# Scattering the experts' results: one copy and plain float32 products in place of two rounded halves

## The chip, the cores and the metric

The kernel runs on one core of one Trainium2 chip. The metric is the time of one execution on the device, in microseconds (us). Before the change it is 1255.69 us, the median of three runs (1255.01 to 1255.78).

## What is computed

Two layers of a decoder trunk on 256 tokens of width 1024. The change touches the second layer's experts: eight SwiGLU networks, of which each token uses two.

```python
logits = (xt @ w_router).astype(jnp.float32)
top_v, top_i = lax.top_k(logits, TOP_K)
gates = jax.nn.softmax(top_v, axis=-1)
gate = jnp.sum(jax.nn.one_hot(top_i, N_EXPERTS, dtype=jnp.float32) * gates[..., None], axis=1)
y = jnp.zeros_like(xt)
for e in range(N_EXPERTS):
    y = y + gate[:, e:e + 1].astype(xt.dtype) * swiglu(xt, wg[e], wu[e], wd[e])
```

with `swiglu(h) = (silu(h @ wg) * (h @ wu)) @ wd`, 1024 to 3584 to 1024. A residual add and a final RMSNorm follow.

## The kernel before, in words

All float32 precision on TensorE comes from halves. A value is split into `hi`, its copy rounded to the type float32r (ScalarE, L145 and L177), and `lo`, the rest (VectorE, L146 and L182). A product of two split operands is three matmuls (`mm3`, L154 to L158). Other products are plain float32 matmuls, without halves.

The experts (`moe`) run on gathered tokens. For each expert a one-hot matrix `pm` (tokens by slots) is built, the tokens are gathered by matmuls with it (`Group.gather`, L625), and the expert's result is scattered back to the tokens by matmuls with its transpose `pT` (`Job.turn_mask`, `evac_mask`). There are two kinds of job, ordered by the number of tokens that fell to an expert:

- **Wide** (5 jobs): up to 128 tokens; its products are split (L158, tile 128*128, three matmuls of 512 columns each). Its result `y` stands in two banks `psS`, one for each half `nb` of the 1024 columns.
- **Narrow** (3 jobs): up to 64 tokens; its products are plain float32 with 64 output columns on the array (L756 up, L772 down, tile 128*64), so that two run side by side. Its result stands in one bank `psA`: rows 0 to 63 hold the first 512 columns, rows 64 to 127 the second.

Each job has seven chunks (512 hidden channels each). `run` lays the chunks of wide and narrow jobs into one list of steps, in the order that a table fixes in the code: a step is one half of a weight piece (1 MB, loaded by SyncE into a ring of 12 buffers). The order is written out by hand on PE, VectorE and ScalarE; each engine takes its instructions strictly as they stand.

After the last chunk of a job the result leaves PSUM and is scattered. `evac_y` (L659) splits it into `yh` (ScalarE) and `yl` (VectorE). `scatter` takes a bank and multiplies both halves by `pT`, adding up in PSUM: for a wide job at L685 with the full array, for a narrow job at L714 with 64 rows, so that the scatters of the two `nb` run side by side. `add` (L667, VectorE) multiplies by the gate and adds to the tokens `xs`. In `run` (L826 to L838) these are placed at the steps after the job's end, `e0`: `evac` of half `nb` at `e0` and `e0+2`, the scatters one step apart (narrow jobs: two in a step), the adds behind them. So the scatters of a job lie between the matmuls of whatever chunk comes next, wide or narrow. There are two `psS` banks: the first two scatters take over those of `y`, the third takes the one that the first `add` gives back, and so on.

The very last job is narrow, with nothing to hide behind. It uses `evac_plain` (L701): one copy of the result, half of it by ScalarE, half by VectorE, and one plain float32 matmul for each scatter (L710).

A part of the program behind a branch (L1035) serves experts with more tokens than their room; it is not entered in these runs.

Of the kernel before, what the change touches and what calls it, by code (L numbers as in the profile page):

```python
# [10 lines left out]
F32 = mybir.dt.float32  # L11
F32R = mybir.dt.float32r
BF16 = mybir.dt.bfloat16
I32 = mybir.dt.int32
AF = mybir.ActivationFunctionType
# [4 lines left out]
P = 128  # L20
# [57 lines left out]
def hybrid_kernel(ctx: ExitStack, tc: tile.TileContext, x_d, xT_d, cst_d, fin_d, router_d,  # L78
                  wpool_d, win_d, wout_d, ffn_d, moe_d, out_d):
    nc = tc.nc  # L80
# [22 lines left out]
    def nm(s):  # L103
        uid[0] += 1
        return f"{s}_{uid[0]}"
# [4 lines left out]
    def bank_a():  # L110
        return bank("A", 4)

    def bank_s():
        return bank("S", 2)
# [59 lines left out]
    def split_evac(*parts):  # L174
        for hi, lo, src, g in parts:
            if g is None:
                nc.scalar.activation(hi, src, AF.Copy)  # L177
            else:
                nc.scalar.activation(hi, src, AF.Copy, scale=g)
        for hi, lo, src, g in parts:  # L180
            if g is None:
                nc.vector.tensor_tensor(lo, src, hi.bitcast(F32), op=ALU.subtract)  # L182
            else:
                nc.vector.scalar_tensor_tensor(lo, src, g, hi.bitcast(F32), op0=ALU.mult, op1=ALU.subtract)  # L184
# [287 lines left out]
    def moe(l, pool, acc, close):  # L472
# [22 lines left out]
        def add(t, nb):  # L495
            v = xs[:, t, nb * 512:(nb + 1) * 512]
            nc.vector.tensor_tensor(v, v, acc[nb, t], op=ALU.add)
# [143 lines left out]
        class Job:  # L641
# [14 lines left out]
                self.pT = pool.tile([P, NT * P], F32R, tag=self.kind + "pT", name=nm("pT"), bufs=1)  # L656
                nc.scalar.activation(self.pT, self.tb[:, 0:NT * P], AF.Copy)

            def evac_y(self, nb):  # L659
                yh = pool.tile([P, 512], F32R, tag="ah", name=nm("yh"), bufs=2)  # L660
                yl = pool.tile([P, 512], F32R, tag="al", name=nm("yl"), bufs=2)
                split_evac((yh, yl, self.y[nb], None))
                self.yp[nb] = yh, yl

            def add(self, nb, t):
                xv = xs[:, t, nb * 512:(nb + 1) * 512]
                nc.vector.scalar_tensor_tensor(xv, self.banks.pop((nb, t)), self.gate_col(t), xv, op0=ALU.mult, op1=ALU.add)  # L667
# [1 line left out]
        class Wide(Job):  # L669
# [4 lines left out]

            def start(self):
                self.y = [bank_s() for nb in range(2)]
                self.yp = {}

            def evac(self, nb):
                self.evac_y(nb)  # L680

            def scatter(self, nb, t):
                b = self.banks[nb, t] = bank_s()
                for i in range(2):
                    nc.tensor.matmul(b, self.pT[:, t * P:(t + 1) * P], self.yp[nb][i], start=i == 0, stop=i == 1)  # L685

        class Narrow(Job):

# [3 lines left out]

            def start(self):
                self.y = [bank_a()]
                self.yp = {}

            def evac(self, nb):
                if nb == 0:
                    self.evac_y(0)

            def evac_plain(self):  # L701
                self.yf = pool.tile([P, 512], F32R, tag="ah", name=nm("yf"), bufs=2).bitcast(F32)
                nc.scalar.activation(self.yf[:, 0:256], self.y[0][:, 0:256], AF.Copy)
                nc.vector.tensor_copy(self.yf[:, 256:512], self.y[0][:, 256:512])

            def scatter(self, nb, t, plain=False):
                b = self.banks[nb, t] = bank_a()
                rows = slice(nb * HP, (nb + 1) * HP)
                if plain:
                    nc.tensor.matmul(b, self.pT[rows, t * P:(t + 1) * P].bitcast(F32), self.yf[rows, :], start=True,  # L710
                                     stop=True)
                    return
                for i in range(2):
                    nc.tensor.matmul(b, self.pT[rows, t * P:(t + 1) * P], self.yp[0][i][rows, :], start=i == 0, stop=i == 1)  # L714

        class Chunk:

# [57 lines left out]
        def run(items, gathers, pieces=(), extra=(), small_ops=iter(())):  # L775


            chunks = [Chunk(job, c) for job, c in items]
# [18 lines left out]
            end = len(steps)  # L797
            before, after = {}, {}
# [7 lines left out]
            for n, ch in enumerate(chunks):  # L806
                b, job = pos["g", n, 0], ch.job
# [18 lines left out]
                if ch.c == NC_E - 1 and not final:  # L826
                    e0 = pos["d", n, 3] + 1
                    for i in range(4):
                        if job.splits:
                            nb, t = divmod(i, 2)  # L830
                            s = e0 + 1 + i
                        else:
                            t, nb = divmod(i, 2)
# [11 lines left out]
                        then(b + 7 + j, lambda j=j, made=made: made[0].gather(j))  # L845
                        at(b + 8 + j, lambda j=j, made=made: made[0].evac(j))

            last = chunks[-1].job
            plain = () if last.splits else (True,)
            for i, f in enumerate([(last.evac, (nb,)) for nb in range(2)] if last.splits else [(last.evac_plain, ())]):  # L850
                before.setdefault(end, []).insert(i, f)
            for when, s, f in extra:
                when = {"at": at, "then": then}[when]
                when(s, f)
# [37 lines left out]
            job = chunks[-1].job  # L892
            for t in range(NT):
                for nb in range(2):
                    job.scatter(nb, t, *plain)
                    job.add(nb, t)


# [136 lines left out]
        with tc.If(n_most > 0):  # L1035
            nc.vector.tensor_scalar(slot[:, :, 0], slot[:, :, 0], float(P), None, op0=ALU.subtract)
            with tc.For_i(0, NE) as e:
# [4 lines left out]
                with tc.If(n_e > 0):  # L1042
                    sg_ = small.tile([P, 2, NT], F32, tag="slot_gate", name="slot_gate")
                    for t in range(NT):
                        nc.vector.tensor_copy(sg_[:, 0, t:t + 1], slot[:, t, ds(e, 1)])
                        nc.vector.tensor_copy(sg_[:, 1, t:t + 1], gate[:, t, ds(e, 1)])
                    job = Wide(lambda c, i: moe_d[ds(e, 1), c, i].rearrange("a p d -> p (a d)"),
                               lambda t: sg_[:, 0, t:t + 1], lambda t: sg_[:, 1, t:t + 1])
# [70 lines left out]
    with tc.tile_pool(name="moe", bufs=2, reuse_waits="tile") as pool, \  # L1119
            tc.tile_pool(name="more", bufs=MORE_BUFS, reuse_waits="tile") as extra:  # L1120
        more.append(extra)
        moe_pool.append(pool)
        moe(1, pool, acc, close)
# [89 lines left out]
```

## Time and profile before

| | |
|---|---|
| median of three runs | 1255.69 us |
| the profiled execution | 1256.09 us |
| its span in the trace | 1254.3 us |
| PE (matmul) busy | 1238.4 us, 99% |
| PE weight loads busy | 971.9 us, 77% |
| VectorE (DVE) busy | 845.5 us, 67% |
| ScalarE (ACT) busy | 704.2 us, 56% |
| DMA, mean over the span | 334 GB/s |

The span is what the profiler saw of the execution, from its first to its last instruction; the execution's own time holds 1.8 us more around it. Matmuls are pipelined, so the time of one record is longer than the distance to the next: what a matmul costs is read from the distance of starts or ends. A float32 matmul of the program stands in the trace as two records, a matmul on rounded halves as one.

### The profile page before, as it was taken

Reading aid. Unit: us, or ns where it says so; the run is one execution under the profiler, and the core shown is the slowest. Engines: PE = TensorE matmul, PEld = TensorE weight load, DVE = VectorE, ACT = ScalarE, POOL = GpSimd, SP = SyncE. Lnnn points to the kernel's source line nnn. Section 1 sums busy time; section 2 is a strip of 40 time slices with the busy share of each in tenths; the row PEclk is TensorE's granted clock in tenths of the full one; section 3 lists DMA queues with packets and bytes.
Section 4 is the critical chain, followed back from the end, with each engine's and each line's share of the span. In section 5 each row is a group of like instructions: output and inputs, shape, how many; then the busy total and the mean of one; then the engine's idle time right before and its main releaser. Section 6 shows DMA issues by size and latency. Waiting matters only on the chain.

```text
span 1254.3 us, 19056 instructions
## 1 busy us (share of the span) xinstructions
PE 1238.4 (99%) x7217; PEld 971.9 (77%) x7217; DVE 845.5 (67%) x1152; ACT 704.2 (56%) x917; POOL 18.1 (1%) x34
## 2 busy tenths in 40 slices
PE   9999999999999999999999999999999999999996
PEld 7989999989987777777777677777777677777772
DVE  5786555556869768676766677765865687567663
ACT  6466444456458756555666556655664565556541
POOL 1010000000000000000000000000000000000000
PEclk9999999999999999999999999999999999999998
DMA  9745555545254999999999999999999999999980
GB/s 367 302 143 197 177 198 188 183 167 202 101 201 159 421 421 421 420 421 421 421 399 421 419 410 406 375 421 421 415 408 421 390 416 420 397 420 421 421 368 36
DMA packets 59428, 418.32 MB, mean 334 GB/s; under 512 B 6848, under 2 KB 6976, under 8 KB 9280
## 3 DMA queue, kind: packets, MB, share of 16 engines
q1 hardware_dynamic: 58464, 415.43, 82.2%
q8 instruction: 58, 0.95, 0.3%
q10 hardware_dynamic: 720, 1.07, 0.2%
q0 software_dynamic: 144, 0.52, 0.1%
q14 instruction: 42, 0.34, 0.1%
HBM read 415.95 MB, written 1.05 MB: 332 GB/s over the span
## 4 chain that ended last, share of the span: by engine, by line
PE 96%; ACT 1%; DVE 1%; issue 0%; DMA 0%; POOL 0%; SPq 0%; ACTq 0%; POOLq 0%
PE psA L158 45%; PE psS L158 25%; PE psA L756 12%; PE psA L772 6%; PE psT L733 2%; PE psT L625 1%; PE psS L685 1%; PE psS L270 1%; ACT hi L145 1%; PE psT L193 0%; DMA raw<-in_win 0%; DVE lo L146 0%; PE psT L318 0%; ACT junk L161 0%; PE psT L380 0%
## 5 line engine op out<-in xcount | busy, mean ns | idle before, releaser
L146 DVE TENSOR_TENSOR lo<-raw,hi 128x1024 fp32r<-128x1024 f32 x534 | 639.8, 1222 | 272.9 <-ACT hi L145 259.9
L145 ACT ACTIVATE hi<-raw 128x1024 fp32r<-128x1024 f32 x534 | 553.2, 1058 | 222.6 <-PE psA L158 123.2
L158 PE MATMUL psA<-hi,xh 128*128 128x512 f32 x560 | 223.6, 399 | 0.1
L158 PE MATMUL psA<-lo,xh 128*128 128x512 f32 x560 | 218.9, 391 | 0.5 <-DVE lo L146 0.5
L158 PE MATMUL psA<-hi,xl 128*128 128x512 f32 x560 | 218.5, 390 | 0.0
L756 PE MATMUL psA<-raw,xn 128*64 128x256 f32 x1344 | 152.0, 381 | 0.0
L756 PEld LDWEIGHTS psA<-raw,xn 128*64 128x64 f32 x1344 | 94.2, 137 | 55.9 <-issue 9.9
L158 PEld LDWEIGHTS psA<-hi,xh 128*128 128x128 f32 x560 | 105.2, 188 | 31.9 <-issue 10.9
L158 PEld LDWEIGHTS psA<-lo,xh 128*128 128x128 f32 x560 | 105.1, 188 | 23.7 <-DVE lo L146 1.2
L158 PEld LDWEIGHTS psA<-hi,xl 128*128 128x128 f32 x560 | 105.3, 188 | 20.5 <-DVE xl L184 0.2
L725 ACT ACTIVATE a<-psA 128x512 f32<-128x512 f32 (+1 forms) x56 | 29.0, 518 | 163.6 <-PE psA L756 146.6
L158 PE MATMUL psS<-hi,ah 128*128 128x512 f32 x280 | 112.2, 401 | 0.0
L158 PE MATMUL psS<-lo,ah 128*128 128x512 f32 x280 | 109.6, 391 | 0.0
L158 PE MATMUL psS<-hi,al 128*128 128x512 f32 x280 | 109.5, 391 | 0.0
L158 PE MATMUL psS<-hh,hi 128*128 128x256 f32 x320 | 89.9, 281 | 0.0
L158 PE MATMUL psS<-hh,lo 128*128 128x256 f32 x320 | 89.9, 281 | 0.0
L158 PE MATMUL psS<-hl,hi 128*128 128x256 f32 x320 | 89.8, 281 | 0.0
L772 PE MATMUL psA<-raw,aT 128*64 128x512 f32 x336 | 76.7, 598 | 0.0
L158 PEld LDWEIGHTS psS<-lo,ah 128*128 128x128 f32 x280 | 52.6, 188 | 12.2
L158 PEld LDWEIGHTS psS<-hh,lo 128*128 128x128 f32 x320 | 61.3, 192 | 0.0
L158 PEld LDWEIGHTS psS<-hi,ah 128*128 128x128 f32 x280 | 52.7, 188 | 10.5 <-issue 0.4
L158 PEld LDWEIGHTS psS<-hi,al 128*128 128x128 f32 x280 | 52.7, 188 | 10.0
(213 smaller groups left out, 1460.8 us busy)
## 6 DMA issues: line engine op xcount, KB each, us to landing
raw<-in_moe SPq DMA_DIRECT2D x336, 1024.0 KB, 10.4
raw<-in_ffn SPq DMA_DIRECT2D x33, 1024.0 KB, 4.9
raw<-in_win SPq DMA_DIRECT2D x14, 1024.0 KB, 4.9
raw<-in_wout SPq DMA_DIRECT2D x8, 1024.0 KB, 10.0
raw<-in_win SPq DMA_DIRECT2D x4, 512.0 KB, 6.9
raw<-in_xT SPq DMA_DIRECT2D x4, 256.0 KB, 6.1
xs<-in_x SPq DMA_DIRECT2D x2, 512.0 KB, 12.0
out<-o ACTq DMA_DIRECT2D x4, 256.0 KB, 2.7
```

What stands on the lines that cost most here:

```text
L145: nc.scalar.activation(hi, v, AF.Copy)
L146: nc.vector.tensor_tensor(lo, v, hi.bitcast(F32), op=ALU.subtract)
L158: nc.tensor.matmul(out, lhs, rhs, start=first and i == 0, stop=last and i == 2)
L270: nc.tensor.matmul(banks[i][:, c0:c0 + k1], q[:, q0:q0 + P], k[:, 0:k1], start=True, stop=True)
L625: nc.tensor.matmul(bank[:, i * 256:i * 256 + self.n], part[:, t, k * P:(k + 1) * P], self.pm[:, t, 0:self.n], start=n == 0, stop=n == 3)
L685: nc.tensor.matmul(b, self.pT[:, t * P:(t + 1) * P], self.yp[nb][i], start=i == 0, stop=i == 1)
L725: nc.scalar.activation(self.a, self.g[:, 0:self.n], AF.Silu)
L733: nc.tensor.transpose(self.tb[:, j * P:(j + 1) * P], self.a[:, j * P:(j + 1) * P], ident)
L756: nc.tensor.matmul(bank[half * HP:(half + 1) * HP, 0:256], self.job.xg[:, k, :], w[:, c:c + 256], start=k == 0, stop=k == NK - 1)
L772: nc.tensor.matmul(y[0][nb * HP:(nb + 1) * HP, :], self.aT[:, c:c + HP], w[:, nb * 512:(nb + 1) * 512], start=first, stop=last)
```

## The change

`evac_y` goes. A wide job's result is copied once: the first 512 columns by ScalarE, the second by VectorE, each into one float32 tile (`yf`). A narrow job's is copied as `evac_plain` did it. Every scatter is one plain float32 matmul of `pT` with `yf`. The last job's special case is no longer special. The matrices are the same: `pT` still has the type float32r and is read as float32.

```diff
--- before.py
+++ after.py
@@ -656,12 +656,6 @@
                 self.pT = pool.tile([P, NT * P], F32R, tag=self.kind + "pT", name=nm("pT"), bufs=1)
                 nc.scalar.activation(self.pT, self.tb[:, 0:NT * P], AF.Copy)
 
-            def evac_y(self, nb):
-                yh = pool.tile([P, 512], F32R, tag="ah", name=nm("yh"), bufs=2)
-                yl = pool.tile([P, 512], F32R, tag="al", name=nm("yl"), bufs=2)
-                split_evac((yh, yl, self.y[nb], None))
-                self.yp[nb] = yh, yl
-
             def add(self, nb, t):
                 xv = xs[:, t, nb * 512:(nb + 1) * 512]
                 nc.vector.scalar_tensor_tensor(xv, self.banks.pop((nb, t)), self.gate_col(t), xv, op0=ALU.mult, op1=ALU.add)
@@ -674,15 +668,18 @@
 
             def start(self):
                 self.y = [bank_s() for nb in range(2)]
-                self.yp = {}
+                self.yf = [None, None]
 
             def evac(self, nb):
-                self.evac_y(nb)
+                self.yf[nb] = pool.tile([P, 512], F32R, tag=("ah", "al")[nb], name=nm("yf"), bufs=2).bitcast(F32)
+                if nb == 0:
+                    nc.scalar.activation(self.yf[nb], self.y[nb], AF.Copy)
+                else:
+                    nc.vector.tensor_copy(self.yf[nb], self.y[nb])
 
             def scatter(self, nb, t):
                 b = self.banks[nb, t] = bank_s()
-                for i in range(2):
-                    nc.tensor.matmul(b, self.pT[:, t * P:(t + 1) * P], self.yp[nb][i], start=i == 0, stop=i == 1)
+                nc.tensor.matmul(b, self.pT[:, t * P:(t + 1) * P].bitcast(F32), self.yf[nb], start=True, stop=True)
 
         class Narrow(Job):
 
@@ -692,26 +689,17 @@
 
             def start(self):
                 self.y = [bank_a()]
-                self.yp = {}
 
             def evac(self, nb):
                 if nb == 0:
-                    self.evac_y(0)
-
-            def evac_plain(self):
-                self.yf = pool.tile([P, 512], F32R, tag="ah", name=nm("yf"), bufs=2).bitcast(F32)
-                nc.scalar.activation(self.yf[:, 0:256], self.y[0][:, 0:256], AF.Copy)
-                nc.vector.tensor_copy(self.yf[:, 256:512], self.y[0][:, 256:512])
-
-            def scatter(self, nb, t, plain=False):
+                    self.yf = pool.tile([P, 512], F32R, tag="ah", name=nm("yf"), bufs=2).bitcast(F32)
+                    nc.scalar.activation(self.yf[:, 0:256], self.y[0][:, 0:256], AF.Copy)
+                    nc.vector.tensor_copy(self.yf[:, 256:512], self.y[0][:, 256:512])
+
+            def scatter(self, nb, t):
                 b = self.banks[nb, t] = bank_a()
                 rows = slice(nb * HP, (nb + 1) * HP)
-                if plain:
-                    nc.tensor.matmul(b, self.pT[rows, t * P:(t + 1) * P].bitcast(F32), self.yf[rows, :], start=True,
-                                     stop=True)
-                    return
-                for i in range(2):
-                    nc.tensor.matmul(b, self.pT[rows, t * P:(t + 1) * P], self.yp[0][i][rows, :], start=i == 0, stop=i == 1)
+                nc.tensor.matmul(b, self.pT[rows, t * P:(t + 1) * P].bitcast(F32), self.yf[rows, :], start=True, stop=True)
 
         class Chunk:
 
@@ -845,10 +833,8 @@
                         then(b + 7 + j, lambda j=j, made=made: made[0].gather(j))
                         at(b + 8 + j, lambda j=j, made=made: made[0].evac(j))
 
-            last = chunks[-1].job
-            plain = () if last.splits else (True,)
-            for i, f in enumerate([(last.evac, (nb,)) for nb in range(2)] if last.splits else [(last.evac_plain, ())]):
-                before.setdefault(end, []).insert(i, f)
+            for nb in range(2):
+                before.setdefault(end, []).insert(nb, (chunks[-1].job.evac, (nb,)))
             for when, s, f in extra:
                 when = {"at": at, "then": then}[when]
                 when(s, f)
@@ -892,7 +878,7 @@
             job = chunks[-1].job
             for t in range(NT):
                 for nb in range(2):
-                    job.scatter(nb, t, *plain)
+                    job.scatter(nb, t)
                     job.add(nb, t)
```

On PE, at the end of the second wide job, the first of its four scatters among the next wide job's up projection; before the change (`psA` is the gate or up bank of the next chunk, `hi`/`lo` the weights, `xh`/`xl` its tokens, `psS` the scatter's bank):

```order
L158 MATMUL psA_6886<-lo_6941,xh_6026 128x512
L685 MATMUL psS_6976<-yh_6956,pT_6062 128x512
L685 MATMUL psS_6976<-yl_6957,pT_6062 128x512
L158 MATMUL psA_6991<-hi_6952,xh_6026 128x512
L158 MATMUL psA_6991<-hi_6952,xl_6027 128x512
L158 MATMUL psA_6991<-lo_6953,xh_6026 128x512
```

Here two rows multiply `pT` by the two halves; three more matmuls on `psA` follow before the next such pair. On PE at the same place with the change:

```order
L158 MATMUL psA_6873<-lo_6928,xh_6018 128x512
L682 MATMUL psS_6961<-yf_6943,pT_6054 128x512
L158 MATMUL psA_6973<-hi_6939,xh_6018 128x512
L158 MATMUL psA_6973<-hi_6939,xl_6019 128x512
L158 MATMUL psA_6973<-lo_6940,xh_6018 128x512
```

The pair with `yh` and `yl` has become one row with `yf`; the matmuls around it, and their number between two scatters, stay.

On VectorE at the same place, from the evacuation of the result to the last add; before the change (`lo` are halves of the next chunk's weights, `aT` a narrow chunk's activations, `xs` the adds):

```order
L182 TENSOR_TENSOR yl_6957<-psS_5687,yh_6956 128x512
L146 TENSOR_TENSOR lo_6967<-raw_6950,hi_6966 128x1024
L146 TENSOR_TENSOR lo_6982<-raw_6979,hi_6981 128x1024
L182 TENSOR_TENSOR yl_6986<-psS_5688,yh_6985 128x512
L146 TENSOR_TENSOR lo_7002<-raw_6979,hi_7001 128x1024
L667 SCALAR_TENSOR_TENSOR xs<-psS_6976,gate_o,xs 128x512
L742 COPY aT_7006<-psT_6903 128x256
L667 SCALAR_TENSOR_TENSOR xs<-psS_6998,gate_o,xs 128x512
L667 SCALAR_TENSOR_TENSOR xs<-psS_7014,gate_o,xs 128x512
L667 SCALAR_TENSOR_TENSOR xs<-psS_7026,gate_o,xs 128x512
```

Here the two subtractions `yl` stand among those for the weights, ahead of the adds. On VectorE with the change:

```order
L146 TENSOR_TENSOR lo_6952<-raw_6937,hi_6951 128x1024
L146 TENSOR_TENSOR lo_6966<-raw_6963,hi_6965 128x1024
L678 COPY yf_6969<-psS_5680 128x512
L146 TENSOR_TENSOR lo_6983<-raw_6963,hi_6982 128x1024
L661 SCALAR_TENSOR_TENSOR xs<-psS_6961,gate_o,xs 128x512
L730 COPY aT_6987<-psT_6890 128x256
L661 SCALAR_TENSOR_TENSOR xs<-psS_6980,gate_o,xs 128x512
L661 SCALAR_TENSOR_TENSOR xs<-psS_6995,gate_o,xs 128x512
L661 SCALAR_TENSOR_TENSOR xs<-psS_7006,gate_o,xs 128x512
```

The subtraction for the first half is gone, that for the second has become a COPY from PSUM. On ScalarE the copy to `yh` of the first half has become the copy to `yf`, and that of the second half is gone.

## Rows read from the trace of the kernel before

**Rows 1.** The page: busy time and share of PE; the chain by engine.

```profile
PE 1238.4 (99%) x7217; PEld 971.9 (77%) x7217; DVE 845.5 (67%) x1152; ACT 704.2 (56%) x917; POOL 18.1 (1%) x34
...
PE 96%; ACT 1%; DVE 1%; issue 0%; DMA 0%; POOL 0%; SPq 0%; ACTq 0%; POOLq 0%
```

**Rows 2.** Waits of PE, whole span: group, releaser, total us, times, longest.

```profile
PE psA L710 <- DVE yf L704: 0.9, 1, 0.9
```

**Rows 3.** Waits of the DMA queue (SPq), whole span, same columns.

```profile
SPq L135 <- DVE lo L146: 616.9, 197, 15.0
```

**Rows 4.** Groups by shape: scatters on PE, count, busy us, mean ns, idle before.

```profile
L685 PE MATMUL psS<-yh,pT 128*128 128x512 f32 x20 | 8.9, 446 | 0.0
...
L685 PE MATMUL psS<-yl,pT 128*128 128x512 f32 x20 | 7.9, 395 | 0.0
...
L714 PE MATMUL psA<-yh,pT 64*128 64x512 f32 x8 | 2.0, 496 | 0.0
L710 PE MATMUL psA<-yf,pT 64*128 64x512 f32 x8 | 2.0, 615 | 0.9 <-DVE yf L704 0.9
...
L714 PE MATMUL psA<-yl,pT 64*128 64x512 f32 x8 | 1.6, 392 | 0.0
```

**Rows 5.** Timeline of PE, second wide job: start us, us, engine, line, shape.

```profile
721.96 0.40 PE L158 MATMUL psA<-lo,xh 128*128 128x512 f32 x1
722.20 0.39 PE L685 MATMUL psS<-yh,pT 128*128 128x512 f32 x1
722.43 0.39 PE L685 MATMUL psS<-yl,pT 128*128 128x512 f32 x1
722.66 0.39 PE L158 MATMUL psA<-hi,xh 128*128 128x512 f32 x1
...
725.64 0.39 PE L158 MATMUL psA<-lo,xh 128*128 128x512 f32 x1
726.01 0.47 PE L685 MATMUL psS<-yh,pT 128*128 128x512 f32 x1
726.31 0.40 PE L685 MATMUL psS<-yl,pT 128*128 128x512 f32 x1
```

**Rows 6.** Timeline of PE, last wide job's scatters among a narrow chunk.

```profile
1224.80 1.08 PE L756 MATMUL psA<-raw,xn 128*64 128x256 f32 x8
1225.82 0.50 PE L685 MATMUL psS<-yh,pT 128*128 128x512 f32 x1
1226.15 0.40 PE L685 MATMUL psS<-yl,pT 128*128 128x512 f32 x1
1226.48 0.44 PE L756 MATMUL psA<-raw,xn 128*64 128x256 f32 x2
```

**Rows 7.** Timeline of PE, the last narrow chunk and its plain scatter.

```profile
1232.48 1.89 PE L772 MATMUL psA<-raw,aT 128*64 128x512 f32 x8
1234.30 0.44 PE L733 MATMUL psT<-cst,a 128*128 128x128 f32 x2
1234.66 5.37 PE L772 MATMUL psA<-raw,aT 128*64 128x512 f32 x24
1240.98 1.99 PE L710 MATMUL psA<-yf,pT 64*128 64x512 f32 x8 [0.94 <-DVE yf L704]
```

**Rows 8.** Timeline of PE, pooling products of the first layer.

```profile
73.00 0.39 PE L158 MATMUL psA<-lo,hh 128*128 128x512 f32 x1
73.23 0.38 PE L380 MATMUL psT<-wpool,up 128*128 128x128 f32 x2
73.37 0.48 PE L158 MATMUL psA<-hi,hh 128*128 128x512 f32 x1
```

**Rows 9.** Groups by shape: copies of the wide results on DVE and ACT.

```profile
L182 DVE TENSOR_TENSOR yl<-psS,yh 128x512 fp32r<-128x512 f32 x10 | 6.9, 687 | 4.6 <-ACT yh L177 4.6
...
L177 ACT ACTIVATE yh<-psS 128x512 fp32r<-128x512 f32 x10 | 5.9, 586 | 8.0 <-PE psS L158 7.8
```

**Rows 10.** Timeline of DVE beside rows 5.

```profile
723.97 1.23 DVE L146 TENSOR_TENSOR lo<-raw,hi 128x1024 fp32r<-128x1024 f32 x1
725.12 0.74 DVE L667 SCALAR_TENSOR_TENSOR xs<-psS,gate_o,xs 128x512 f32<-128x512 f32 x1
725.78 0.41 DVE L742 COPY aT<-psT 128x256 f32<-128x256 f32 x1
726.11 1.40 DVE L667 SCALAR_TENSOR_TENSOR xs<-psS,gate_o,xs 128x512 f32<-128x512 f32 x2
```

## The prediction

> **What bounds the kernel now.** I read the page first: TensorE (PE) is busy 1238.4 us of the 1254.3 us span, and the chain that ended last runs 96% through PE [rows 1]. The reader should see that a microsecond added to PE is added to the end, unless PE stands waiting somewhere. So the second view is PE's own waits: eight groups of at most 1.0 us each, none of them on a DMA; the second largest is the 0.9 us behind the last chunk's copy, which the change leaves alone [rows 2]. The third view is the DMA queue's waits: SyncE waits 616.9 us for VectorE to give a weight buffer back [rows 3]. The loads run ahead of the work and stand at full buffers, so a later PE gives them more room, and nothing there swallows what PE gets longer. The fourth view is the timeline of PE around the scatters, and the fifth the groups by shape, for the counts.
>
> **What a scatter costs now.** The five wide jobs have 20 scatters of two matmuls, 20 records with yh and 20 with yl; the first two narrow jobs have 8 scatters with 8 yh records, which run side by side in pairs (each uses 64 rows), so 4 places [rows 4]. The last narrow job already uses the plain product and stays. Reading the timeline around each scatter, 12 of the 20 wide places (the second to the fourth wide job) lie between matmuls of the same 128*128 shape, 8 (the first and the last wide job) between the 128*64 matmuls of a narrow chunk; of the 4 narrow places 2 lie among 128*64 matmuls and 2 among 128*128 ones.
>
> Between 128*128 matmuls a half follows a half after 0.23 us (722.20, 722.43, 722.66), so a place costs 2 x 0.23 = 0.46 [rows 5]. Between 128*64 matmuls it costs more: the group before ends at 1224.80 + 1.08 = 1225.88, the first pair after ends at 1226.48 + 0.44 = 1226.92, 1.04 later, of which 0.22 is the pair itself: 0.82 for the place [rows 6]. That is 0.46 for the halves and 0.36 for changing the tile shape from 128*64 to 128*128 and back.
>
> **What a float32 product costs.** The plain scatter of the last job is 4 instructions in the program and 8 records in the trace, so a float32 product is two passes [rows 7]. Its passes, and those of the float32 down projection, are slow: 24 records of L772 stand in pairs, 12 passes of 512 columns, in 5.37 us, hence about 0.43 a pass if the last one's drain of some 0.2 is set aside; the 8 of L710 make 4 passes in 1.99 [rows 7]. Two passes are 0.86. No row shows a float32 product of the full 128*128 array with 512 columns. I bound a pass from both sides by the nearest rows: 0.43 (float32, 512 columns, but half tiles in pairs) and 0.23 (512 columns of the full array, but rounded operands [rows 5]). I take 0.43, since the element type is what the change changes: a pair of half-array products takes 0.43 a pass in float32 (L710 [rows 7]), while L685 of the full array takes 0.23 in the rounded type.
>
> Does changing the element type cost anything by itself? Between full-array matmuls no: L158 ends at 73.39, the two records of L380 (true float32, 128*128) end at 73.61, and the next L158 at 73.85, 0.24 later, the usual 0.23 [rows 8]. Does the change of tile shape stay when both sides are float32? Yes: L772 (128*64) ends at 1234.37, the two transposes L733 (float32, 128*128) end at 1234.74; 0.37 less two of 0.11 leaves 0.15 on the way in. On the way out, L772 ends at 1240.03, 5.29 after the transposes, against 12 x 0.43 = 5.16: 0.13 [rows 7, 8]. So 0.28 instead of 0.36.
>
> **The sum on PE.** Twelve wide places among 128*128 matmuls: 0.86 - 0.46 = +0.40 each, +4.8. Twelve among other shapes (8 wide, 4 narrow; I price the narrow ones alike, since their pairs run side by side in both versions): 0.86 + 0.28 - 0.82 = +0.32, or +0.40 if the exchange stays at 0.36; I take +0.35, +4.2. Together +9.0.
>
> The FP8 and Floating Point Precision page of the Trainium skill (TensorE Precision Notes) says that true FP32 makes four passes through the array; with this case's 0.23 for a pass a product would be 0.92, and the sum would be about 1.4 us more than mine. The trace shows two records of 0.43 each, so about the same work in another form; the rows decide.
>
> **What the copies give back.** ScalarE loses five of its ten 0.59 us copies out of PSUM, and VectorE's ten 0.69 us subtractions become five plain copies [rows 9]: some 6.4 us of the two engines, nearly all beside PE's work and worth nothing. One wait hangs on it. In the second to the fourth wide job the third scatter needs the bank that the first add releases. VectorE is late there: a lo half runs from 723.97 to 725.20, the add from 725.12 to 725.86 [rows 10], and the scatter starts at 726.01, 0.37 after the matmul before it instead of 0.23, and is itself 0.08 longer: 0.22 lost [rows 5]. With the change one subtraction is gone from VectorE's queue, and PE reaches this place two scatters x 0.40 later, at about 726.7: the add is done long before. Three such places: -0.66. What is late next there is PE itself: the adds wait for longer products, but the scatter that reuses a bank comes six matmuls (1.4 us) after the add could start, and an add is 0.74 [rows 10].
>
> Moved steps: none. Order, loads and queues stay; SyncE and POOL issue what they did. The ah and al buffers are used by fewer tiles, which costs nothing (fewer owners, same two buffers). The program's tail after the last chunk is untouched.
>
> **Sum:** 4.8 + 4.2 - 0.66 = +8.3 us. The profiled execution took 1256.09 us, 0.40 above the median of 1255.69; on the median that makes 1264.0.
>
> **The rivals.**
> 1. A full-array float32 pass takes 0.23, because the 0.43 of rows 7 is two half tiles sharing a path. For it: all 0.43 rows are pairs, and the only full-array float32 passes, 0.11 for 128 columns [rows 8], may be held by their weight loads and not by the columns. Against: the halves of L714 run in pairs too, 8 records each of 0.50 and less, shorter than L710's 0.62 [rows 4]. Then the 12 places cost 0, the 8 wide others 0.46 + 0.28 - 0.82 = -0.08, the 4 narrow still +0.35: -0.6 + 1.4 - 0.66 = +0.1, 1255.8: not slower. It turns to "no change" (2.5 us) at a pass of about 0.29. Chance 0.05.
> 2. The bitcasts do not do what the words say, and a scatter stays one record of 0.23: 24 x -0.23 - 0.66 = -6.2, 1249.5, faster. Against: L710 has the same bitcasts and two passes. Chance 0.02.
> 3. The exchange of 0.28 to 0.36 belongs to the element type, not the shape, and vanishes among float32 neighbours: 10 places at 0.86 - 0.82 = +0.04, 2 at +0.35, 12 at +0.40: 0.4 + 0.7 + 4.8 - 0.66 = +5.2, 1260.9. Against: L772 to L733 is float32 on both sides and pays [rows 7]. Chance 0.08.
> 4. VectorE, which works in order, stands behind adds that wait for longer scatters, and the halves behind them come late: up to two scatters x 0.40 in each of the same three jobs, +2.4: 1266.4. For it: the adds of these jobs already come back to back [rows 10]. Against: the pieces after them are the narrow chunk's, which need no halves. Chance 0.10.
>
> **How the numbers follow.** The forecast's own case, +7.2 to +9.6 (the exchange at either price, the three waits gone or kept), has 0.75. The range reaches from rival 3 to rival 4, 1260.9 to 1266.4, and leaves out rivals 1 and 2. A measurement of this kernel can tell some 0.2%, 2.5 us: faster 0.02 (rival 2), the same 0.05 (rival 1), slower 0.93.
>
> **What would show it.** In the profile after: the scatter line of the wide job with 40 records of some 0.6 us (two per product), the next L158 about 0.86 + 0.23 after the matmul before; the narrow one with 16 more records; no gap before the third scatter; PE's busy time up by 8 to 9 us with the span, ScalarE and VectorE down by some 3 us each. One record per product, or a spacing of 0.23 between the two, makes the forecast wrong; so does a new PE wait of more than a microsecond on VectorE in the scatter stages.

## The result, and the profile after

The changed kernel takes 1264.47 us, the median of six runs (1264.33 to 1264.61), beside 1255.74 us for the kernel before in six runs (1255.01 to 1256.01): 8.7 us slower, a ratio of 1.0071 [1.006, 1.0081]. Forecast were 1264.0 us and a range of 1260.9 to 1266.4. The profiled execution after took 1264.54 us and its span is 1262.8 us, 8.5 us longer than that of before.

The page of the kernel after: its span, the busy times, and the chain by engine.

```profile
span 1262.8 us, 19039 instructions
...
PE 1245.7 (99%) x7217; PEld 971.3 (77%) x7217; DVE 842.5 (67%) x1147; ACT 701.1 (56%) x912; POOL 18.1 (1%) x34
...
PE 96%; ACT 1%; DVE 1%; issue 1%; DMA 0%; POOL 0%; SPq 0%; ACTq 0%; POOLq 0%
```

Beside [rows 1]: PE is busy 7.3 us longer, ScalarE 3.1 and VectorE 3.0 us less, and the chain still runs 96% through PE. The two relieved engines were not the bound, the one that got longer was. PE has the same 7217 matmul records: a product that was two matmuls on rounded halves is now one float32 matmul, and that stands in the trace as two records.

The groups by shape of the kernel after: the scatters of the wide and of the narrow jobs on PE, and the copies on VectorE and ScalarE.

```profile
L682 PE MATMUL psS<-yf,pT 128*128 128x512 f32 x40 | 21.3, 613 | 0.0
L661 DVE SCALAR_TENSOR_TENSOR xs<-psS,gate_o,xs 128x512 f32<-128x512 f32 x16 | 12.0, 748 | 13.4 <-PE psS L682 13.4
L702 PE MATMUL psA<-yf,pT 64*128 64x512 f32 x24 | 6.5, 632 | 0.9 <-DVE yf L697 0.9
L678 DVE COPY yf<-psS 128x512 f32<-128x512 f32 x5 | 3.4, 687 | 4.7 <-PE psS L158 4.7
L676 ACT ACTIVATE yf<-psS 128x512 f32<-128x512 f32 x5 | 2.9, 587 | 7.8 <-PE psS L158 7.8
```

Twenty wide scatters make 40 records, as before [rows 4], but of 613 ns on the mean where the halves had 446 and 395. Of ten copies on each engine five are left, and a single one takes as long as it did [rows 9].

The timeline of PE of the kernel after, second wide job: the place of [rows 5].

```profile
723.71 0.40 PE L158 MATMUL psA<-lo,xh 128*128 128x512 f32 x1
723.94 1.02 PE L682 MATMUL psS<-yf,pT 128*128 128x512 f32 x2
724.40 0.80 PE L158 MATMUL psA<-hi,xh 128*128 128x512 f32 x1
...
728.21 0.40 PE L158 MATMUL psA<-lo,xh 128*128 128x512 f32 x1
728.45 1.02 PE L682 MATMUL psS<-yf,pT 128*128 128x512 f32 x2
```

The two records begin 0.43 us apart: 1.02 for both, less 0.59 for one. The L158 ahead of the first place ends at 723.71 + 0.40 = 724.11, the one behind at 724.40 + 0.80 = 725.20. These 1.09 us are the product and that L158, of which the latter is 0.23: 0.86 for the scatter, where it was 0.46. The lower two rows are the third scatter. It begins 0.24 us after the matmul ahead of it; in [rows 5] that was 0.37, with a wait in it.

The timeline of PE of the kernel after, last wide job: the place of [rows 6].

```profile
1232.11 1.08 PE L744 MATMUL psA<-raw,xn 128*64 128x256 f32 x8
1233.13 1.12 PE L682 MATMUL psS<-yf,pT 128*128 128x512 f32 x2
1234.18 0.44 PE L744 MATMUL psA<-raw,xn 128*64 128x256 f32 x2
```

From the end of the group ahead (1233.19) to the end of the first pair behind (1234.62) pass 1.43 us, less 0.22 for the pair: 1.21 for the place, where [rows 6] gave 0.82. So +0.39, of which 0.86 - 0.46 = 0.40 is the product: the change of tile shape still costs its 0.36 (1.21 less 0.86 makes 0.35).

The waits of PE of the kernel after, whole span: engine and line that waited, for whom, us in total, times, longest.

```profile
PE psA L158 <- DVE lo L146: 1.0, 2, 0.5
PE psS L1083 <- DVE zero L1080: 1.0, 1, 1.0
PE psA L702 <- DVE yf L697: 0.9, 1, 0.9
...
PE psA L158 <- ACT hi L145: 0.6, 1, 0.6
```

No wait among the scatters came in. The waits of L158, two for `lo` and one for `hi`, lie ahead of 540 us, before the first scatter, in code that the change leaves alone; the 0.9 us behind the last chunk is the one of [rows 2].

### The profile page after: what moved, and what is told of

Same layout as the page of the kernel before. It is cut to its first block, busy times and chain, and to the rows that moved or that the text cites. A ratio compares the mean times of both kernels' runs of the same rounds, so it can differ in the third digit from the quotient of the medians.

```text
span 1262.8 us, 19039 instructions
## 1 busy us (share of the span) xinstructions
PE 1245.7 (99%) x7217; PEld 971.3 (77%) x7217; DVE 842.5 (67%) x1147; ACT 701.1 (56%) x912; POOL 18.1 (1%) x34
## 4 chain that ended last, share of the span: by engine, by line
PE 96%; ACT 1%; DVE 1%; issue 1%; DMA 0%; POOL 0%; SPq 0%; ACTq 0%; POOLq 0%
PE psA L158 44%; PE psS L158 25%; PE psA L744 12%; PE psA L760 6%; PE psT L721 2%; PE psS L682 1%; PE psT L625 1%; PE psS L270 1%; ACT hi L145 1%; PE psT L193 0%; PE psA L702 0%; DMA raw<-in_win 0%; DVE lo L146 0%; PE psT L318 0%; ACT junk L161 0%
## 5 line engine op out<-in xcount | busy, mean ns | idle before, releaser
L158 PE MATMUL psA<-hi,xh 128*128 128x512 f32 x560 | 228.5, 408 | 0.1
L158 PE MATMUL psA<-lo,xh 128*128 128x512 f32 x560 | 219.1, 391 | 0.5 <-DVE lo L146 0.5
L158 PE MATMUL psA<-hi,xl 128*128 128x512 f32 x560 | 218.5, 390 | 0.0
L158 PEld LDWEIGHTS psA<-hi,xh 128*128 128x128 f32 x560 | 105.2, 188 | 35.1 <-issue 12.9
L158 PEld LDWEIGHTS psA<-lo,xh 128*128 128x128 f32 x560 | 105.1, 188 | 23.8 <-DVE lo L146 1.2
L158 PEld LDWEIGHTS psA<-hi,xl 128*128 128x128 f32 x560 | 105.4, 188 | 23.0 <-issue 2.9
L158 PE MATMUL psS<-hi,ah 128*128 128x512 f32 x280 | 112.2, 401 | 0.0
L158 PE MATMUL psS<-lo,ah 128*128 128x512 f32 x280 | 109.6, 391 | 0.0
L158 PE MATMUL psS<-hi,al 128*128 128x512 f32 x280 | 109.5, 391 | 0.0
L158 PE MATMUL psS<-hh,hi 128*128 128x256 f32 x320 | 89.9, 281 | 0.0
L158 PE MATMUL psS<-hh,lo 128*128 128x256 f32 x320 | 89.9, 281 | 0.0
L158 PE MATMUL psS<-hl,hi 128*128 128x256 f32 x320 | 89.8, 281 | 0.0
L158 PEld LDWEIGHTS psS<-lo,ah 128*128 128x128 f32 x280 | 52.6, 188 | 12.2
L158 PEld LDWEIGHTS psS<-hh,lo 128*128 128x128 f32 x320 | 61.3, 192 | 0.0
L158 PEld LDWEIGHTS psS<-hi,ah 128*128 128x128 f32 x280 | 52.7, 188 | 10.5 <-issue 0.4
L158 PEld LDWEIGHTS psS<-hi,al 128*128 128x128 f32 x280 | 52.7, 188 | 10.0
```

What stands on the lines that cost most here:

```text
L158: nc.tensor.matmul(out, lhs, rhs, start=first and i == 0, stop=last and i == 2)
```

## The experiments

Theory A in the expectations is the forecast's own: the scatter's price on PE (a pass of 0.43, two to a product), the price of the tile's shape, and a wait at the third scatter of three jobs. Where the figures of a single place are given (0.39, 0.41 and 0.17 for `wide_only`), they are read from the trace of the kernel after, so there the agreement tests that the parts add up, and not the prices. What is set against it is told in each text; A2 is the theory on that wait that was formed after the run `one_pass`. "Place" is a scatter with what it costs around itself. The times of before are those taken beside each run on the same chip.

**One kind of job at a time.** `wide_only` is the kernel before with the new `evac` and `scatter` of the wide jobs; `narrow_only` has those of the narrow jobs and leaves the wide ones with halves.

```diff
# wide_only, against before
-                self.evac_y(nb)
+                self.yf[nb] = pool.tile([P, 512], F32R, tag=("ah", "al")[nb], name=nm("yf"), bufs=2).bitcast(F32)
+                if nb == 0:
+                    nc.scalar.activation(self.yf[nb], self.y[nb], AF.Copy)
+                else:
+                    nc.vector.tensor_copy(self.yf[nb], self.y[nb])
...
-                for i in range(2):
-                    nc.tensor.matmul(b, self.pT[:, t * P:(t + 1) * P], self.yp[nb][i], start=i == 0, stop=i == 1)
+                nc.tensor.matmul(b, self.pT[:, t * P:(t + 1) * P].bitcast(F32), self.yf[nb], start=True, stop=True)
# narrow_only, against before
-                    self.evac_y(0)
+                    self.yf = pool.tile([P, 512], F32R, tag="ah", name=nm("yf"), bufs=2).bitcast(F32)
+                    nc.scalar.activation(self.yf[:, 0:256], self.y[0][:, 0:256], AF.Copy)
+                    nc.vector.tensor_copy(self.yf[:, 256:512], self.y[0][:, 256:512])
...
-                    nc.tensor.matmul(b, self.pT[rows, t * P:(t + 1) * P], self.yp[0][i][rows, :], start=i == 0, stop=i == 1)
+                nc.tensor.matmul(b, self.pT[rows, t * P:(t + 1) * P].bitcast(F32), self.yf[rows, :], start=True, stop=True)
```

Expected of `wide_only`:

> The wide jobs alone get the copy and the plain product; the narrow jobs keep the halves. Theory A (all of the change is TensorE's time at the 24 places, less three waits): 8 places x 0.39, 9 x 0.41 and 3 x 0.17 make +7.3 us, about 1263.1. Theory B (a good part comes from the other copies and VectorE's order, not from the products): the wide jobs' share differs from 7.3 by more than 1 us and the two single changes do not add up to the whole +8.7.

Measured: 1263.02 us beside 1255.67, ratio 1.0058 [1.0041, 1.0075], +7.35 us.

Expected of `narrow_only`:

> The first two narrow jobs alone get the copy and the plain product. Theory A: 4 places x 0.40 make +1.6 us, about 1257.3. Theory B: since the copy of a narrow result is ready 0.5 us earlier than its halves, a gain shows, and the time is nearer to that of before, below 1256.5.

Measured: 1257.54 us beside 1255.67, ratio 1.0014 [1.0005, 1.0024], +1.9 us. The two parts together make +9.2 where the whole change made +8.7. So they add up within half a microsecond, and a narrow place costs about as much as a wide one: 1.9 / 4 = 0.47 by these medians, 0.39 in the timeline of the kernel after, where the first narrow scatter among 128*64 matmuls takes 1.18 us in place of 0.79 (from the end of the group ahead to the end of the eight matmuls behind, less four pairs of 0.22).

**The same lighter copies, with cheap products.** `one_pass` keeps all of the change, its copies and its order, but the copies round and the products are in the rounded type: one matmul of 0.23 for each scatter, those of the last narrow job too. It leaves out the low halves of the experts' results.

```diff
# one_pass, against after (the narrow jobs alike)
-                self.yf[nb] = pool.tile([P, 512], F32R, tag=("ah", "al")[nb], name=nm("yf"), bufs=2).bitcast(F32)
+                self.yf[nb] = pool.tile([P, 512], F32R, tag=("ah", "al")[nb], name=nm("yf"), bufs=2)
...
-                nc.tensor.matmul(b, self.pT[:, t * P:(t + 1) * P].bitcast(F32), self.yf[nb], start=True, stop=True)
+                nc.tensor.matmul(b, self.pT[:, t * P:(t + 1) * P], self.yf[nb], start=True, stop=True)
```

> The copies and the order of the changed kernel, but the copy and the one-hot matrix are multiplied in the rounded type, in one record for each scatter. This leaves out the low half of every expert's result but the last narrow one's, whose scatter now takes the rounded type too. Theory A: each of the 24 places loses one pass of 0.23 against before, and the three waits go: 24 x -0.23 - 0.66 = -6.2, some 0.9 more in the last narrow job's tail (two passes of 0.43 twice against one of 0.23 twice: -1.2): 1248.2 to 1249.6. Theory B (the copies or the order cost by themselves): 1251 or more.

Measured: 1251.46 us beside 1255.67, ratio 0.9967 [0.9954, 0.9979]. That misses A's figure by about 2 us and lies on B's side, so where PE stood has to be read from the trace. The timeline of PE of `one_pass`, second wide job: the first, the second and the third scatter.

```profile
720.29 0.40 PE L682 MATMUL psS<-yf,pT 128*128 128x512 f32 x1
...
721.91 0.47 PE L682 MATMUL psS<-yf,pT 128*128 128x512 f32 x1
...
723.37 0.39 PE L158 MATMUL psA<-lo,xh 128*128 128x512 f32 x1
724.01 0.50 PE L682 MATMUL psS<-yf,pT 128*128 128x512 f32 x1 [0.25 <-DVE xs L661]
724.35 0.40 PE L158 MATMUL psA<-hi,xh 128*128 128x512 f32 x1
```

The third scatter begins 0.64 us after the matmul ahead of it, not 0.23. From the end of that matmul (723.76) to the end of the one behind the scatter (724.75) pass 0.99 us, where one pass and one matmul are 0.46: about 0.5 lost, more than the 0.22 of the kernel before, although VectorE has one subtraction less to do. The waits of PE of `one_pass` count three such places, one in each of the three jobs (their totals hold the visible idle time alone):

```profile
PE psS L682 <- DVE xs L661: 0.8, 3, 0.3
```

And the timeline of VectorE of `one_pass` beside it:

```profile
722.07 1.22 DVE L146 TENSOR_TENSOR lo<-raw,hi 128x1024 fp32r<-128x1024 f32 x1 [0.25 <-ACT hi L145]
723.21 0.74 DVE L661 SCALAR_TENSOR_TENSOR xs<-psS,gate_o,xs 128x512 f32<-128x512 f32 x1
```

The add, whose bank the third scatter takes over, stands behind a `lo` half on VectorE. That half cannot start earlier: VectorE waits 0.25 us ahead of it for ScalarE's `hi`. The subtraction that went away therefore did not bring the add forward: in the kernel before, in `one_pass` and in the kernel after it ends 3.66 us after the first scatter began (722.20 to 725.86, 720.29 to 723.95, 723.94 to 727.60; the same, to 0.01, in the other two jobs). The wait's length is set by when PE arrives, and in `one_pass` PE arrives one matmul earlier for each of two scatters. In the kernel after it arrives later, 4.51 us after the first scatter (728.45), and finds the add done. This is A2: the wait goes because PE is late, not because VectorE is relieved. So B is right in so far as the order of the add costs `one_pass` its gain; that a copy costs anything by itself is not seen. A part of the miss lies elsewhere: A counted some 0.9 to 1.2 us for the last narrow job, and from the start of its scatter to the end of the span there are 13.0 us where there were 13.3.

**The add ahead of the half.** To test A2, `halves_early_add` takes the kernel before, with its halves, and moves only the first add one place forward on VectorE, in the three jobs that another wide chunk follows. `one_pass_early` makes the same edit in `one_pass`.

```diff
-                        at(e0 + 3 + i, job.add, nb, t)
+                        if job.splits and i == 0 and chunks[steps[e0][1]].job.splits:
+                            then(e0 + 2, job.add, nb, t)
+                        else:
+                            at(e0 + 3 + i, job.add, nb, t)
```

> The kernel before, with halves; only the first add of a wide job that is scattered among wide matmuls stands one place earlier on VectorE, ahead of a lo half of the weights. Theory A (the three waits of 0.22 come from that add being late): the gap before the third scatter goes in the three jobs, -0.66 us, about 1255.1, within the noise of the time but plain in the timeline. Rival D (the wait moves to the weights' half that now stands behind the add): the third scatter starts on time, but a matmul on that half waits, and the time is that of before or above.

Measured: 1254.76 us beside 1255.56, ratio 0.9994 [0.9985, 1.0003]: -0.8 us, as expected, in an interval that still holds no change, though all eleven runs (1254.56 to 1254.90) lie below all 21 of the kernel before (1255.35 to 1256.00). What shows the cause is the trace. The timeline of VectorE of `halves_early_add`, second wide job:

```profile
722.23 0.69 DVE L182 TENSOR_TENSOR yl<-psS,yh 128x512 fp32r<-128x512 f32 x1
722.83 0.74 DVE L667 SCALAR_TENSOR_TENSOR xs<-psS,gate_o,xs 128x512 f32<-128x512 f32 x1
723.49 1.22 DVE L146 TENSOR_TENSOR lo<-raw,hi 128x1024 fp32r<-128x1024 f32 x1
```

And its timeline of PE at the third scatter:

```profile
724.72 0.40 PE L158 MATMUL psA<-lo,xh 128*128 128x512 f32 x1
724.96 0.39 PE L685 MATMUL psS<-yh,pT 128*128 128x512 f32 x1
725.19 0.39 PE L685 MATMUL psS<-yl,pT 128*128 128x512 f32 x1
```

The add now stands ahead of the half, the scatter begins 0.24 us after the matmul ahead of it, and the first half is 0.39 long and no more 0.47: the wait of [rows 5] is gone with nothing taken from VectorE.

> As one_pass (a single product in the rounded type for each scatter, without the low half), but the first add of a wide job that is scattered among wide matmuls stands one place earlier on VectorE. Theory A2 (the wait before the third scatter is the add's place behind a lo half, and it is as long as TensorE is early; the lighter copies do nothing for it): the three gaps of 0.52 close, -1.6 against one_pass, about 1249.9. Theory B (the shortfall of one_pass against its forecast is a cost of the copies): no change, 1251.5.

Measured: 1249.66 us beside 1255.83, ratio 0.9952 [0.9939, 0.9966], 1.8 us below `one_pass`. Of that, the three places that had lost 0.52 each make 1.6. The rest, 0.2, is within the spread of the runs; at the second scatter the trace still has a first record of 0.46 (0.47 in `one_pass`), so nothing came back there. The timeline of PE of `one_pass_early`, second wide job, third scatter:

```profile
723.10 0.39 PE L158 MATMUL psA<-lo,xh 128*128 128x512 f32 x1
723.33 0.39 PE L682 MATMUL psS<-yf,pT 128*128 128x512 f32 x1
723.56 0.39 PE L158 MATMUL psA<-hi,xh 128*128 128x512 f32 x1
```

The pass is 0.23 from its neighbours on both sides, where the third scatter of `one_pass` began 0.64 after the matmul ahead. A2 stands.

**The tile's shape.** `plain_half_tiles` is the kernel after, with the wide scatters that lie among narrow chunks cut into two products of 64 output columns. These have the 128*64 shape of the matmuls around them, and stay float32.

```diff
+            beside = False
...
-                nc.tensor.matmul(b, self.pT[:, t * P:(t + 1) * P].bitcast(F32), self.yf[nb], start=True, stop=True)
+                n = 2 if self.beside else 1
+                for h in range(n):
+                    c = slice(h * HP, (h + 1) * HP) if self.beside else slice(0, P)
+                    nc.tensor.matmul(b[c, :], self.pT[:, t * P + c.start:t * P + c.stop].bitcast(F32), self.yf[nb],
+                                     start=True, stop=True)
...
+                    job.beside = not chunks[steps[e0][1]].job.splits
```

> The changed kernel, but the wide scatters that lie among a narrow chunk's matmuls are cut into two products of 64 output columns each, the shape of their neighbours. Theory A (the 0.36 at such a place belongs to the change of tile shape): the two run side by side in 2 x 0.43 without an exchange, 7 places x -0.35, about -2.5 against the changed kernel: 1262.0. Theory C (the 0.36 belongs to the element type or to any new product): unchanged, 1264.5. If the two do not run side by side: 8 x 0.86 more less the exchange, about 1269.

Measured: 1262.46 us beside 1255.67, ratio 1.0053 [1.0036, 1.0069], 2.0 us below the 1264.47 of the change. The timeline of PE of `plain_half_tiles`, last wide job:

```profile
1231.41 1.03 PE L749 MATMUL psA<-raw,xn 128*64 128x256 f32 x8
1232.28 1.03 PE L686 MATMUL psS<-yf,pT 128*64 128x512 f32 x4
1233.14 0.39 PE L749 MATMUL psA<-raw,xn 128*64 128x256 f32 x2
```

From 1232.44 to 1233.53 are 1.09 us, less 0.22 for the pair: 0.87 for the place, which is the product's 0.86 and nothing for an exchange. Against 1.21 in the kernel after, that is 0.34 at each of seven places, 2.4 in all (behind the eighth, the first scatter of the first wide job, stand 128*128 transposes); the medians give 2.0, where about 2.5 was expected. The element type was float32 on both sides in both kernels, so the price belongs to the shape. Cutting the halves of the kernel before in the same way was not tried.

**Scatters of one shape side by side.** If the shape costs 0.36 on the way in and out, two scatters that follow each other pay it once. `halves_paired` is `halves_early_add` with the scatters of the first and the last wide job placed two and two; the copies of the second half come a step earlier for that, and the adds follow. The early add stays as it was for the other three jobs.

```diff
# against halves_early_add
                         if i % 2 == 0:
-                            at(e0 + i, job.evac, i // 2)
+                            early = job.splits and not chunks[steps[e0][1]].job.splits
+                            at(e0 + (i // 2 if early else i), job.evac, i // 2)
+                        paired = job.splits and not chunks[steps[e0][1]].job.splits
+                        if paired:
+                            s = e0 + 2 + 3 * nb
                         then(s, job.scatter, nb, t)
+                        if paired:
+                            at(s + 1 + t, job.add, nb, t)
...
```

> As the run with the early add, and in the two wide jobs that are scattered among a narrow chunk two scatters stand in one step, so that their tile shape is entered once for two. Theory A: three exchanges of 0.36 less (the first job's first scatter shared one with the transposes beside it), -1.1, and the three waits, -0.66: about -1.7, 1254.0. Theory C (the 0.36 belongs to each product and not to the change of shape): -0.66 alone, 1255.1. A new wait for a bank or an add in the paired steps would give it back.

Measured: 1253.5 us beside 1255.56, ratio 0.9984 [0.9975, 0.9993]: 2.1 us faster than the kernel before, and 1.3 less than `halves_early_add`. The timeline of PE of `halves_paired`, last wide job:

```profile
1222.13 0.82 PE L756 MATMUL psA<-raw,xn 128*64 128x256 f32 x6
1222.88 0.50 PE L685 MATMUL psS<-yh,pT 128*128 128x512 f32 x1
1223.22 0.39 PE L685 MATMUL psS<-yl,pT 128*128 128x512 f32 x1
1223.44 0.40 PE L685 MATMUL psS<-yh,pT 128*128 128x512 f32 x1
1223.68 0.39 PE L685 MATMUL psS<-yl,pT 128*128 128x512 f32 x1
1224.00 1.30 PE L756 MATMUL psA<-raw,xn 128*64 128x256 f32 x10
```

The four half products follow each other at 0.22 to 0.34. From 1222.95 to 1225.30 pass 2.35 us, less five pairs of 0.22: 1.25 for two scatters, where two single places were 2 x 0.82 = 1.64. That is 0.39 for an exchange, and three of them go (the first job's first scatter had shared one with the transposes beside it), so 1.2; 1.3 came. Whole results are scattered here, as in the kernel before, and this version is faster than both kernels, by 0.2% and 0.9%.

`one_pass_paired` is `one_pass_early` with the same pairs; like `one_pass` it leaves out the low halves.

> As one_pass_early, and in the first and the last wide job two scatters stand in one step. Theory A: three exchanges of tile shape of 0.36 less, -1.1, about 1248.8; with single passes the paired scatters leave VectorE less time for the adds, and a wait of some tenths before the second pair could give a part back.

Measured: 1248.86 us beside 1255.83, ratio 0.9946 [0.9932, 0.9959]. It is 0.8 us below `one_pass_early`; the pairs work there too. Against their own runs of before, it gains 7.0 us and `halves_paired` 2.1, so 4.9 lie between them. The second half of every scatter would be 24 x 0.23 = 5.5 on PE; in the traces the stretch from the first scatter to the end of the last wide one is 4.8 us shorter (671.9 beside 676.7), since at some places less came back: 0.3 of it is a wait for ScalarE's `a` behind a narrow job's scatter, which all three `one_pass` runs show and the kernel before does not. The last narrow job's scatter, rounded in these runs alone, gives 0.6 more (12.8 beside 13.4 from its start to the end of the span), and the first scatter began 0.5 later in the profiled execution of `one_pass_paired`.

## Why the prediction was right

**What bounds.** PE, as read from the page [rows 1]: 6 us of copies went from two engines and brought nothing, and every microsecond added to PE came out at the end. The queue of weight loads swallowed none of it: SyncE waits 618.6 us for VectorE's halves after the change, where [rows 3] had 616.9.

**The price of a pass.** The forecast took 0.43 us for a float32 pass of the full array, from rows of half tiles only [rows 7]. The trace shows 0.43, in two records for each of the 20 products. That fells rival 1 (0.23) and rival 2 (one record), which held 0.07 between them. The FP8 and Floating Point Precision page of the Trainium skill (TensorE Precision Notes) speaks of four passes. This trace has two records of 0.43 where a rounded product has 0.23, and how many passes a record holds it does not show; the 1.4 us that four passes of 0.23 would have added, an estimate from that page's count, are not there.

**The twelve places among 128*128 matmuls.** Foretold +0.40 each; measured +0.40 in the rows above, and 0.41 on the mean of nine. At the three third scatters the place grew by 0.17, since the wait that was in it is gone: the +0.40 less the forecast's 0.22.

**The twelve at a change of shape.** This term was under-sized. The forecast let the exchange fall from 0.36 to 0.28 when both sides are float32 (the sum of 0.15 in and 0.13 out around the transposes L733 [rows 7]) and took +0.35 a place, 4.2 in all. Measured: +0.39 at the eight wide places and +0.39 to +0.41 at the four narrow ones, so 4.7 in all, and 0.5 too little was foretold. The forecast placed eight wide scatters between 128*64 matmuls; the first of them has 128*128 transposes behind it, and it grew by 0.39 like the others. The upper end of that step, +0.40, was the better reading: the products of the same width, the halves of [rows 6], were nearer to the case than transposes of 128 columns.

| term | foretold, us | measured, us |
|---|---|---|
| 12 places among 128*128, waits aside | +4.8 | 9 x 0.41 + 3 x 0.40 = +4.9 |
| 12 places at a change of shape | +4.2 | 8 x 0.39 + 4 x 0.40 = +4.7 |
| three waits | -0.66 | 3 x (0.17 - 0.40) = -0.7 |
| sum | +8.3 | +8.9 |

From the start of the first scatter to the end of the last wide one, the traces have 679.0 us before (550.9 to 1229.9) and 688.1 after (550.3 to 1238.4): +9.1. The span grew by 8.5 only, since the first scatter began 0.6 us earlier in the profiled execution of after. Nothing ahead of it was changed; over the eight profiles without pairs that start lies between 550.0 and 550.9. So sum and median agree better (8.3 beside 8.7) than the terms do, which is in part luck. The lower end of the forecast's own case is a slip, too: it stands as +7.2, and its terms make 4.8 + 12 x 0.32 - 0.66 = +8.0; the result lies above both.

**The three waits.** The size was right, and half of the reason was wrong. The forecast gave two causes: one subtraction less in VectorE's queue, and PE arriving 0.8 us later. `one_pass` has the first without the second, and its wait is longer, not gone; the add ends 3.66 us after the first scatter began with the subtraction and without it. `halves_early_add` removes it by order alone. Only the second cause is borne out.

**Rival 3**, that the exchange belongs to the element type, had 0.08 and falls: among float32 neighbours the place still pays (1.21), and with half tiles of the same type it does not (0.87).

**Rival 4** foresaw VectorE standing behind adds that wait for longer scatters. The first half of it happened, the second did not. The timeline of VectorE of the kernel after, second wide job:

```profile
726.86 0.74 DVE L661 SCALAR_TENSOR_TENSOR xs<-psS,gate_o,xs 128x512 f32<-128x512 f32 x1
...
727.85 0.74 DVE L661 SCALAR_TENSOR_TENSOR xs<-psS,gate_o,xs 128x512 f32<-128x512 f32 x1
729.51 0.75 DVE L661 SCALAR_TENSOR_TENSOR xs<-psS,gate_o,xs 128x512 f32<-128x512 f32 x1 [0.92 <-PE psS L682]
731.77 0.75 DVE L661 SCALAR_TENSOR_TENSOR xs<-psS,gate_o,xs 128x512 f32<-128x512 f32 x1 [1.51 <-PE psS L682]
```

The last two adds wait 0.92 and 1.51 us, where the kernel before had the second and third back to back [rows 10] and a wait of 1.09 ahead of the fourth; over the span these sixteen adds of four wide jobs wait 13.4 us for their scatter, where it was 7.2. Yet no wait of PE for VectorE stands in the scatter stages, so this idle time cost nothing.

**The signs** that were named came: two records a product, 16 more at the narrow scatter (24 for 8), no gap at the third one, ScalarE and VectorE down by 3.1 and 3.0. PE's busy time rose by 7.3 where 8 to 9 was named, by less than the span.

## What to carry to other kernels

Where PE is the bound, count what a change costs PE before what it saves elsewhere: here a plain float32 product took 0.86 us where two rounded ones took 0.46 for 512 columns, and the copies saved on two other engines brought nothing. Count the changes of tile shape on PE, and put products of one shape side by side: that alone gave 1.3 us here, with the halves kept. And when a wait goes because the waiter comes later, it is still in the order; here it returned, larger, when the waiter was made faster, and what removed it was to move the late operation, not to lighten the queue that it stands in.

## What was not expected of the hardware

A change between the tile shapes 128*64 and 128*128 cost PE some 0.35 us in and out, whatever the element type: 0.36 with rounded halves between plain products, 0.35 with float32 on both sides, 0.34 saved when the shape is kept (`plain_half_tiles`). The 64*128 products of the narrow jobs pay as well among 128*128 ones: 0.40 at one such place and 0.5 at the other, in both kernels. Changing the type between products of the same shape cost nothing that the trace resolves: 0.24 from L158 to the first float32 record, where a neighbour of the same type comes after 0.23.

The weight loads (PEld) show what differs at such a place. Timelines of PEld and PE of the kernel before, second and last wide job:

```profile
721.97 0.19 PEld L685 LDWEIGHTS psS<-yh,pT 128*128 128x128 f32 x1
...
1227.49 0.19 PEld L685 LDWEIGHTS psS<-yh,pT 128*128 128x128 f32 x1 [0.39 <-issue]
...
1227.49 0.50 PE L685 MATMUL psS<-yh,pT 128*128 128x512 f32 x1
```

Timeline of PEld of `plain_half_tiles`, last wide job:

```profile
1232.06 0.36 PEld L686 LDWEIGHTS psS<-yf,pT 128*64 128x64 f32 x4
```

Among matmuls of its own shape the scatter's weights are loaded 0.23 us ahead of the product (721.97 for the one at 722.20 [rows 5]); behind a 128*64 matmul the load begins with the product itself (1227.49), after 0.39 us in which nothing was loaded and nothing that the profile shows was waited for. With half tiles it is ahead again, by 0.22 (1232.06 for 1232.28). At the entry of all twelve places with a change of shape, in both kernels, the load begins with the product. Whether the late load is the whole of the 0.35 is not tested.
